# Feed-forward of a diffusion-transformer layer on one core: the hi and lo parts of four quarters of the gated features are made in the first stage and kept in DRAM

## The chip, the core and the metric

The kernel runs on one core of a Trainium2 chip. A core has a matrix engine (PE, with its weight loads shown apart as PEld), a vector engine (DVE), an activation engine (ACT), a general engine (POOL), a queue engine that issues the transfers (SP), and 16 DMA engines that carry them. The metric is the device time of one execution in microseconds; the median over several runs counts, and lower is better.

## The reference, cut to what matters

One layer (attention, then a gated feed-forward) over 1024 tokens plus 256 context tokens, in float32, width 1024; the hidden width of the feed-forward is 2816. The attention does not change. The part at hand is

```
FFN_HIDDEN = -(-8 * D_MODEL // (3 * 256)) * 256      # 2816

def _swiglu(h, w_ffn_in, w_ffn_out):
    gate, up = jnp.split(h @ w_ffn_in, 2, axis=-1)
    return (jax.nn.silu(gate) * up) @ w_ffn_out
```

Behind it come the gated residual and a last RMS norm over the 1024 features of every token.

## The kernel before, in words

**Three products for one.** A float32 matrix product is made from three fast ones: each operand is split into a high part (rounded to the fast format, `ACT.activation(hi, src, Copy)`, L344) and a low part (`DVE.tensor_tensor(lo, src, hi, subtract)`, L347), and hi·hi, hi·lo and lo·hi are summed in PSUM. So each block of 128x512 that becomes an operand costs one ACT and one DVE instruction; this is `split`.

**Seven products for eight.** Both feed-forward matrices are worked in quarters with a seven-product scheme (`p1` to `p7`). Some products take a quarter as it is, others take sums or differences of quarters, which POOL and DVE make first.

**First stage (class `Hidden`).** The hidden width is cut into 22 chunks `j` of 128. Each j has seven products of 12 matmuls (`product`, L1427). Two weight tiles `wf` of 512 KB are loaded ahead and split. At `p7` DVE (L1528, L1532, L1533) and POOL (L1532, L1533) make two gated halves `hd` [128 x 512], one for each half of the tokens; for j below 11 POOL subtracts the first from the second (L1537). Each half is stored in DRAM (`hidD`, L1538). j = 0 and 1 are written out by hand in program order (`manual_schedule`); from j = 2 on only PE's order is that of the program, and a scheduler places the instructions of DVE, ACT, POOL and SP.

**Output stage.** The products come in the order p1, p5, p2, p6, p3, p7, p4. Each runs over 11 chunks of the hidden width, and over 4 blocks of output features (`chunk_product`, L1713): 132 matmuls, 12 for a chunk. The chunks are prepared in pairs (6 pairs, the last has one chunk), three pairs ahead of their use. `prepare(name, s)` takes the left side (`left`: weights of `w_ffn_out`, loaded raw by L1635 into a ring of 512 KB tiles named wf, wh and wl) and the right side (`right`: a raw pair of `hidD` halves), and splits every chunk of either side into blocks `wh, wl, xh, xl` from a ring of 32, which is eight chunks' worth. For p5 POOL sums two raw weights into `Y` (L1662) and the right side goes into a tile `X` that is kept (L1678). For p6 POOL takes a raw weight from `Y` (L1666) and DVE makes `X` the difference of a raw half and `X` (L1682). For p3 and p7 POOL subtracts `Y` from a raw weight (L1669); for p7 and p4 DVE subtracts the raw half from `X` (L1685). p4 keeps its left parts in the `Y` tiles and a ring tile.

**What follows a product.** `take` reads the four PSUM banks: residual sums on DVE (L1728 `res`), copies on ACT, sums `y` on POOL (L1750), squares on ACT (L1298) that POOL adds up (`acc`, L1300) for the norm. After p2 POOL also scales 256-column pieces of `res` ahead of the norm (`prescale`, L1760). `stat` (L1310) sums the squares on PE in the midst of p4, after the eighth chunk of its first two feature blocks; `spread_stat` (L1321) spreads the result.

**What sets the order.** Each engine works off its instructions in order, so one that waits holds up all behind it. SP issues all transfers that matter here, also in order: a store that waits for its data holds up the loads behind it. A transfer also waits for the one issued eight places before it on SP, as they share eight semaphores.

Of the kernel before, what the change touches and what calls it, by code (L numbers as in the profile page):

```python
# [305 lines left out]
def tile_hybrid_diffattn_mla_dit_layer(  # L306
# [78 lines left out]
    VB = dram.tile([10, P, HB * 128], F32, name="VB")  # L385
    nlD = dram.tile([D, NL], F32, name="nlD")
    hidD = dram.tile([NJ, P, NL], F32, name="hidD")

    def fetch_w(src, width, kk=8):

# [1031 lines left out]
    def product(ps, w, name):  # L1422

        for k in range(4):
            xh, xl = parts[(*name, k)]
            for i, (a, b) in enumerate(((w[0], xh), (w[0], xl), (w[1], xh))):
                PE.matmul(ps, a[:, k, :], b, start=k == 0 and i == 0, stop=k == 3 and i == 2)  # L1427

    class Hidden:


# [93 lines left out]
        def p7(self):  # L1525
            d = mm_tile()
            product(d, self.s3, ("T3",))
            DVE.tensor_tensor(self.v, self.v, d, ALU.add)  # L1528
            both = []
            for i, (eng, other, op, gate) in enumerate(((DVE, self.e, ALU.subtract, self.sg0), (POOL, self.v5, ALU.add, self.sg1))):  # L1530
                hd = self.tile("hd", 3)
                eng.tensor_tensor(hd, self.v, other, op)  # L1532
                eng.tensor_tensor(hd, hd, gate, ALU.mult)  # L1533
                both.append(hd)
                if i and self.j < NJ // 2:
                    hd = self.tile("hd", 3)
                    POOL.tensor_tensor(hd, both[1], both[0], ALU.subtract)  # L1537
                dma(hidD[self.j, :, i * 512:i * 512 + 512], hd)  # L1538

    p4, pk = ExitStack(), ExitStack()  # L1540
    with tc.manual_schedule(engines=ENGINES):
# [68 lines left out]
            h.p4()  # L1610
        for h in first:
            h.p7()
    for j in range(2, NJ - 1):
        h, ahead = ahead, Hidden(j + 1)
        for step in ("p1", "p5", "p2", "p6", "p3", "p4", "p7"):
            getattr(h, step)()

# [26 lines left out]
    def hidden(a, b, s, tag=None):  # L1646
        return raw(hidden_src(a, b, s), pairs[s][1], tag)
# [24 lines left out]
    def right(name, s):  # L1672

        n = pairs[s][1]
        last = name == "p4" and ("wf", "raw")[s % 2]
        if name == "p5":
            X[s] = sum_tile("X", n)
            dma(X[s], hidden_src(0, 1, s))  # L1678
            return X[s]
        r = hidden(*{"p1": (0, 0), "p2": (1, 0), "p6": (1, 1), "p3": (1, 1), "p7": (0, 0), "p4": (1, 0)}[name], s, last)  # L1680
        if name == "p6":
            DVE.tensor_tensor(X[s], r, X[s], ALU.subtract)  # L1682
            return X[s]
        if name in ("p7", "p4"):
            DVE.tensor_tensor(r, X[s], r, ALU.subtract)  # L1685
        return r

    ready = {}

    def prepare(name, s):  # L1690

        c, n = pairs[s]
        a, b = left(name, s), right(name, s)
        if name == "p4":
            hi = sum_tile("Y", n, F32R)
            tag = RAW[2 + s % 2]
            lo = ring.tile([P, 8, P], F32R, tag=tag, name=tag, bufs=3).rearrange("p a b -> p (a b)")
            lo = lo.rearrange("p (c t) -> p c t", c=2)
        for i in range(n):
            wh, wl = (hi[:, i], lo[:, i]) if name == "p4" else (block(), block())  # L1700
            split(wh, wl, a[:, i])
            xh, xl = block(), block()
            split(xh, xl, b[:, i])
            ready[name, c + i] = wh, wl, xh, xl

    def chunk_product(name, c, ps, ds, t0=0):
# [72 lines left out]
    AHEAD = 3  # L1779
    for step in ("p1", "p2", "p5", "p6", "p3", "p4", "p7"):  # L1780
        getattr(ahead, step)()
        if step in ("p2", "p5"):
            prepare(*todo.pop(0))
        if step == "p3":
            pk.close()
            fo2 = pool(ctx, "fo2", side="right")
    p4.close()
    fo = pool(ctx, "fo")
    while len(todo) > len(order) * len(pairs) - AHEAD:
# [110 lines left out]
```

## Time and the profile before

| | |
|---|---|
| median of 3 runs | 1641.59 us (1640.61 to 1644.83) |
| the profiled execution | 1640.7 us, its span 1638.9 us, mean granted clock 0.978 |
| PE busy | 1519.1 us, 93% of the span |
| DVE, ACT, POOL busy | 1193.3, 759.6, 798.5 us |
| first stage | until 1391.95 us |
| output stage | from 1391.95 us to the end |

The span runs from the first instruction to the last of one execution; the profiled time is 1.8 us longer. A granted clock of 1.00 is 2.4 GHz on PE, 0.5 would be 1.2 GHz.

### The profile page before, as it was taken

To read this page: it belongs to the slowest core of one execution; us is meant where nothing else is said; L and a number is where in the kernel's file an instruction comes from. 1 tells how busy PE (TensorE), PEld (TensorE's weight loads), DVE (VectorE), ACT (ScalarE), POOL (GpSimd) and SP (SyncE) were. 2 spreads that over 40 slices of the span, in tenths; PEclk is the share of its full clock that TensorE was granted. 3 is DMA by queue.
4 is the path that set the end of the run, shared out by engine and by line. 5 is a ranking of instruction groups with operands and counts; after the bars stand their busy time and mean duration, and the time that the engine had idled before them with its cause. 6 is when DMAs were issued, how large, how long until landed. Compare 5 with 4: busy or idle time off the path is not lost.

```text
span 1638.9 us, 20678 instructions
## 1 busy us (share of the span) xinstructions
PE 1519.1 (93%) x7323; PEld 1214.8 (74%) x7323; DVE 1193.3 (73%) x1642; ACT 759.6 (46%) x1192; POOL 798.5 (49%) x551
## 2 busy tenths in 40 slices
PE   4899999987778899999999989999999999999887
PEld 2577888765566678788877857888888888888766
DVE  5757565579999988999975588655555556869893
ACT  5443421265556557677764444333333333444251
POOL 2435335435656656755622275755544441437531
PEclk8999999999999999999999989999999999999997
DMA  8436987592332345453217412322222225963432
GB/s 252 138 96 223 319 280 226 186 265 87 84 90 72 71 97 142 110 157 82 65 52 212 154 45 71 110 90 84 77 84 78 77 78 185 369 235 136 159 116 103
DMA packets 153923, 227.70 MB, mean 139 GB/s; under 512 B 11215, under 2 KB 80859, under 8 KB 153819
## 3 DMA queue, kind: packets, MB, share of 16 engines
q1 hardware_dynamic: 153547, 226.11, 44.7%
q8 instruction: 58, 0.95, 0.2%
q14 instruction: 46, 0.38, 0.1%
q10 hardware_dynamic: 272, 0.26, 0.0%
HBM read 172.53 MB, written 53.81 MB: 138 GB/s over the span
## 4 chain that ended last, share of the span: by engine, by line
PE 58%; DVE 23%; DMA 6%; issue 4%; POOL 4%; ACT 3%; SPq 1%; DVEq 0%; ACTq 0%; POOLq 0%
PE mm L1427 24%; PE mm L1713 8%; PE S L1056 7%; DVE nm L1076 4%; PE T L1118 4%; DVE nm L1072 4%; PE mm L1355 3%; DVE pl L1126 3%; PE acc L1135 2%; DVE block L347 2%; PE acc L1140 2%; PE mm L410 2%; PE mm L600 1%; DVE nmc L1068 1%; PE ps L1355 1%
## 5 line engine op out<-in xcount | busy, mean ns | idle before, releaser
L1090 ACT ACTIVATE e<-S,nm 128x1280 f32<-128x1280 f32 x128 | 170.1, 1329 | 104.3 <-DVE nm L1076 79.9
L1056 PE MATMUL S<-kt,qt 128*128 128x512 f32 (+1 forms) x768 | 200.9, 370 | 13.6 <-ACT e L1090 11.4
L1713 PE MATMUL mm<-block 128*128 128x512 f32 x792 | 182.0, 392 | 6.8 <-DVE block L347 6.8
L1118 PE MATMUL T<-ident,e 128*128 128x128 f32 x960 | 147.8, 277 | 36.1 <-DVE pl L1126 32.1
L1713 PEld LDWEIGHTS mm<-block 128*128 128x128 f32 x792 | 149.5, 189 | 39.1 <-DVE block L347 8.1
L1122 ACT ACTIVATE ph<-T 128x512 fp32r<-128x512 f32 x240 | 142.1, 597 | 75.8 <-PE T L1118 71.7
L1118 PEld LDWEIGHTS T<-ident,e 128*128 128x128 f32 x960 | 115.1, 142 | 77.6 <-issue 29.9
L1126 DVE TENSOR_TENSOR pl<-T,ph 128x512 fp32r<-128x512 f32 x240 | 161.3, 682 | 15.0 <-ACT ph L1122 12.5
L1056 PEld LDWEIGHTS S<-kt,qt 128*128 128x128 f32 x768 | 132.2, 192 | 49.6 <-ACT e L1090 26.3
L1072 DVE TENSOR_REDUCE nm<-S 128x1 f32<-128x1024 f32 x128 | 155.8, 1217 | 15.6 <-PE S L1056 14.3
L1110 POOL TENSOR_SCALAR e<-e,ls 128x1280 f32<-128x1280 f32 x64 | 85.9, 1342 | 116.5 <-DVE ls L1107 101.0
L1135 PE MATMUL acc<-ph,vt 128*128 128x512 f32 x320 | 131.1, 450 | 2.0 <-ACT ph L1122 1.1
L1427 PE MATMUL mm<-fresh,wh 128*128 128x512 f32 x352 | 113.8, 402 | 3.3 <-DVE fresh L1580 2.9
L1427 PE MATMUL mm<-block,wh 128*128 128x512 f32 x352 | 112.3, 400 | 0.0
L1532 POOL TENSOR_TENSOR hd<-acc,v 128x512 f32<-128x512 f32 x22 | 29.6, 1344 | 147.3 <-DVE acc L1528 135.7
L344 ACT ACTIVATE wh<-wf 128x1024 fp32r<-128x1024 f32 (+1 forms) x51 | 52.2, 1026 | 103.6 <-issue 64.1
L1140 PE MATMUL acc<-pl,vt 128*128 128x512 f32 x240 | 99.3, 414 | 0.0
L1300 POOL TENSOR_TENSOR acc<-acc,sq 128x512 f32<-128x512 f32 x23 | 35.2, 1530 | 129.6 <-ACT sq L1298 129.0
L410 PE MATMUL mm<-hH,wh 128*128 128x512 f32 (+1 forms) x256 | 95.2, 372 | 0.0
L1104 POOL TENSOR_TENSOR e<-e,e 128x1280 f32<-128x1280 f32 x32 | 93.6, 2926 | 2.7
L410 PE MATMUL mm<-hH,wl 128*128 128x512 f32 (+1 forms) x256 | 93.9, 367 | 0.0
L410 PE MATMUL mm<-hL,wh 128*128 128x512 f32 (+1 forms) x256 | 93.8, 366 | 0.0
(367 smaller groups left out, 3705.5 us busy)
## 6 DMA issues: line engine op xcount, KB each, us to landing
wf<-in_w_ffn_in_dram SPq DMA_DIRECT2D x44, 512.0 KB, 3.8
hidD<-hd SPq DMA_DIRECT2D x44, 256.0 KB, 2.1
wh<-in_w_ffn_out_dram SPq DMA_DIRECT2D x21, 512.0 KB, 5.9
wl<-hidD SPq DMA_DIRECT2D x17, 512.0 KB, 6.5
wa<-in_w_ada_dram SPq DMA_DIRECT2D x16, 512.0 KB, 4.0
wa<-in_w_ada_dram SPq DMA_DIRECT2D x32, 256.0 KB, 3.7
qt<-QB SPq DMA_DIRECT2D x32, 256.0 KB, 4.4
qt<-QA SPq DMA_DIRECT2D x32, 256.0 KB, 4.9
```

Source lines behind the costliest of these rows:

```text
L410: PE.matmul(ps, a(k), b(k), start=start and i == 0, stop=stop and i == n - 1)
L1056: m = PE.matmul(S[:, c0:c0 + w], q, k[:, k0:k0 + w], start=s == 0, stop=s == len(job) - 1)
L1072: on_banks(DVE.tensor_reduce(self.stats(n)[0][:, i:i + 1], sl, AX.X, ALU.max, negate=True), BANKS[i], DVE)
L1090: m = ACT.activation(e, S[:, i * NT:(i + 1) * NT], AF.Exp, bias=self.s[n][0][:, i:i + 1], accum_out=total)
L1104: POOL.tensor_tensor(self.e[n, 0], self.e[n, 0], self.e[n, 1], ALU.add)
L1118: PE.transpose(self.T[c][:, b * P:(b + 1) * P], e[:, kc * P:(kc + 1) * P], ident)
L1122: ACT.activation(self.ph[c], self.T[c], AF.Copy)
L1126: DVE.tensor_tensor(self.pl[c], self.T[c], f32(self.ph[c]), ALU.subtract)
L1135: PE.matmul(self.acc[u, qh, j], vt[:, kc, v], self.ph[c], start=kc == 0 and i == 0, stop=False)
L1140: PE.matmul(self.acc[u, qh, j], self.kv[u][1][:, kc, v], self.pl[c], start=False, stop=kc == 9)
L1427: PE.matmul(ps, a[:, k, :], b, start=k == 0 and i == 0, stop=k == 3 and i == 2)
L1713: PE.matmul(ps[d], w[:, sl], x[:, t0:t0 + n], start=c == 0 and i == 0, stop=c == NH - 1 and i == 2)
```

## The change

The kept DRAM tile `hidS` gets, for each of the 44 halves `hd`, its high and low part side by side. A new function `split_late` makes them with one `split` into a tile `hs` of two blocks and stores it (512 KB). It is called after p1 and after p5 of the next j; for j = 0 and 1 it stands right behind each `p7`, within the part that is ordered by hand; for the last j it is called after p1, p5 and p7. `hd` has two buffers instead of three, as POOL now subtracts in place.

In the output stage p1, p2, p5 and p3 take quarters of the features as they are (`PLAIN`). For these `prepare` loads `xh` and `xl` straight from `hidS` into blocks (two transfers of 256 KB for a chunk) and splits nothing on that side. p6, p7 and p4 take differences and are as before; `X` is still loaded for p5.

```
+    hidS = dram.tile([NJ, P, 2, 2, 512], F32, name="hidS")
...
+    late = []
+
+    def split_late():
+
+        if late:
+            hd, dst = late.pop(0)
+            hs = ff.tile([P, 2, 512], F32R, tag="hs", name="hs", bufs=1)
+            split(hs[:, 0], hs[:, 1], hd)
+            dma(dst, f32(hs))
...
-                hd = self.tile("hd", 3)
+                hd = self.tile("hd")
                 eng.tensor_tensor(hd, self.v, other, op)
                 eng.tensor_tensor(hd, hd, gate, ALU.mult)
                 both.append(hd)
                 if i and self.j < NJ // 2:
-                    hd = self.tile("hd", 3)
-                    POOL.tensor_tensor(hd, both[1], both[0], ALU.subtract)
+                    POOL.tensor_tensor(hd, hd, both[0], ALU.subtract)
                 dma(hidD[self.j, :, i * 512:i * 512 + 512], hd)
+                late.append((hd, hidS[self.j, :, i]))
...
         for h in first:
             h.p7()
+            while late:
+                split_late()
...
             getattr(h, step)()
+            if step in ("p1", "p5"):
+                split_late()
...
-        if name == "p5":
-            X[s] = sum_tile("X", n)
-            dma(X[s], hidden_src(0, 1, s))
-            return X[s]
-        r = hidden(*{"p1": (0, 0), "p2": (1, 0), "p6": (1, 1), "p3": (1, 1), "p7": (0, 0), "p4": (1, 0)}[name], s, last)
+        r = hidden(*{"p6": (1, 1), "p7": (0, 0), "p4": (1, 0)}[name], s, last)
...
+    PLAIN = {"p1": (0, 0), "p2": (1, 0), "p5": (0, 1), "p3": (1, 1)}
...
-        a, b = left(name, s), right(name, s)
+        a = left(name, s)
+        if name == "p5":
+            X[s] = sum_tile("X", n)
+            dma(X[s], hidden_src(0, 1, s))
+        if name not in PLAIN:
+            b = right(name, s)
...
             xh, xl = block(), block()
-            split(xh, xl, b[:, i])
+            if name in PLAIN:
+                half, i2 = PLAIN[name]
+                for p, t in enumerate((xh, xl)):
+                    dma(f32(t), hidS[half * NH + c + i, :, i2, p])
+            else:
+                split(xh, xl, b[:, i])
...
         getattr(ahead, step)()
+        if step in ("p1", "p5", "p7"):
+            split_late()
...
+    while late:
+        split_late()
     p4.close()
```

In total 44 splits leave the output stage and 44 enter the first one, so the engines' instruction counts stay the same (1056 activations, 1044 two-operand DVE instructions, 7142 matmuls). SP issues 750 transfers instead of 636: 44 stores of 512 KB and 88 loads of 256 KB come in, and 18 raw loads of `hidD` (8.25 MiB) fall away.

How the change moves the rows is shown at three places. The line numbers of the changed kernel are 12 to 24 higher (L1528 became L1540, L1666 became L1682, L1760 became L1784).

First DVE, where j = 0 and 1 end and j = 2 begins. `acc` (L1528) adds p7's bank, `hd` (L1532, L1533) makes the gated half, `wl`, `sl` and `ul` are low parts of weights, `y` is the gate of j = 2. Before:

```order
L1528 TENSOR_TENSOR acc<-acc,mm 128x512
L347 TENSOR_TENSOR wl<-wf,wh 128x1024
L1532 TENSOR_TENSOR hd<-acc,mm 128x512
L1533 TENSOR_TENSOR hd<-hd,y 128x512
L1528 TENSOR_TENSOR acc<-acc,mm 128x512
L1532 TENSOR_TENSOR hd<-acc,mm 128x512
L347 TENSOR_TENSOR ul<-wf,uh 128x512
L1533 TENSOR_TENSOR hd<-hd,y 128x512
```

And in the changed kernel:

```order
L1540 TENSOR_TENSOR acc<-acc,mm 128x512
L347 TENSOR_TENSOR wl<-wf,wh 128x1024
L1544 TENSOR_TENSOR hd<-acc,mm 128x512
L1545 TENSOR_TENSOR hd<-hd,y 128x512
L347 TENSOR_TENSOR hs<-hd,hs 128x512
L347 TENSOR_TENSOR ul<-wf,uh 128x512
L347 TENSOR_TENSOR sl<-s_9274,sh 128x1024
L1511 TENSOR_TENSOR y<-acc,mm 128x512
L347 TENSOR_TENSOR wl<-s_9275,wh 128x1024
L347 TENSOR_TENSOR hs<-hd,hs 128x512
L1540 TENSOR_TENSOR acc<-acc,mm 128x512
```

The second `acc`, that of j = 1, which frees its PSUM bank, now stands behind both `hs` of j = 0 and behind four instructions that belong to j = 2.

Next SP at the passage from the first stage to the output stage, in the changed kernel: `hidS<-hs` are the stores of the last parts, `block<-hidS` the loads of p1's and then p5's right side, `X`, `wf`, `wh`, `wl` raw loads of p5.

```order
L1651 DMA wl<-in_w_ffn_out_dram 128x2x512
L1549 DMA hidD<-hd 128x512 x2
L1439 DMA hidS<-hs 128x1024
L1725 DMA block<-hidS 128x512 x4
L1439 DMA hidS<-hs 128x1024
L1725 DMA block<-hidS 128x512 x3
L1744 DMA res<-nlD 128x2x512 x2
L1725 DMA block<-hidS 128x512
L1710 DMA X_12363<-hidD 128x2x512
L1725 DMA block<-hidS 128x512 x4
L1651 DMA wf<-in_w_ffn_out_dram 128x2x512 x2
```

Before, two stores of `hidD` stood here among raw loads; now two stores of `hidS` do as well, and the last of them stands ahead of p1's last blocks and of all of p5's.

Last POOL from p6's differences to p3's. Before:

```order
L1666 TENSOR_TENSOR Y_12445<-Y_12445,wh 128x512
L1669 TENSOR_TENSOR wf<-wf,Y_12203 128x1024
L1669 TENSOR_TENSOR wh<-wh,Y_12251 128x1024
L1669 TENSOR_TENSOR wh<-wh,Y_12299 128x1024
L1669 TENSOR_TENSOR wh<-wh,Y_12349 128x1024
L1760 TENSOR_SCALAR res<-res,fnorm 128x256 x2
L1300 TENSOR_TENSOR acc<-acc,sq 128x512
L1760 TENSOR_SCALAR res<-res,fnorm 128x256 x2
```

And in the changed kernel:

```order
L1682 TENSOR_TENSOR Y_12453<-Y_12453,wh 128x1024
L1784 TENSOR_SCALAR res<-res,fnorm 128x256 x2
L1302 TENSOR_TENSOR acc<-acc,sq 128x512
L1784 TENSOR_SCALAR res<-res,fnorm 128x256 x2
L1302 TENSOR_TENSOR acc<-acc,sq 128x512
L1784 TENSOR_SCALAR res<-res,fnorm 128x256
L1302 TENSOR_TENSOR acc<-acc,sq 128x512
L1784 TENSOR_SCALAR res<-res,fnorm 128x256
L1682 TENSOR_TENSOR Y_12503<-Y_12503,wh 128x1024
L1682 TENSOR_TENSOR Y_12551<-Y_12551,wf 128x1024
L1682 TENSOR_TENSOR Y_12599<-Y_12599,wh 128x512
```

Before, all six differences of p6 and four of p3 were made ahead of the scaling and the sums of squares that belong to p2's results; now the differences of p6's pairs 3 to 5 stand behind them.

## Rows read from the trace of the kernel before

**Rows 1.** The page, part 1: busy time, share, instructions of each engine.

```profile
PE 1519.1 (93%) x7323; PEld 1214.8 (74%) x7323; DVE 1193.3 (73%) x1642; ACT 759.6 (46%) x1192; POOL 798.5 (49%) x551
```

**Rows 2.** Windows: stretch, length, busy time by engine, PE clock, DMA share, GB/s.

```profile
1160.00:1200.00 40.00, 40.00 (x175) 32.64 (x174) 22.30 (x25) 13.01 (x17) 21.23 (x15) 1.00 0.26 88
...
1392.00:1422.00 30.00, 30.00 (x134) 24.86 (x133) 25.36 (x26) 13.70 (x25) 17.26 (x8) 1.00 1.00 363
1422.00:1453.00 31.00, 31.00 (x139) 25.67 (x138) 18.57 (x28) 15.79 (x29) 2.09 (x2) 1.00 0.81 291
1453.00:1483.00 30.00, 30.00 (x134) 24.86 (x133) 27.21 (x22) 11.88 (x21) 16.70 (x7) 1.00 0.61 204
1483.00:1514.00 31.00, 31.00 (x139) 25.67 (x138) 31.00 (x33) 15.74 (x28) 27.37 (x14) 1.00 0.39 142
1514.00:1545.00 31.00, 25.51 (x107) 20.66 (x106) 25.73 (x31) 7.65 (x14) 13.70 (x7) 0.94 0.46 160
...
1599.00:1639.00 40.00, 31.81 (x167) 27.45 (x167) 15.24 (x34) 5.59 (x12) 6.92 (x9) 0.80 0.30 105
```

**Rows 3.** Timeline of PE, output stage: start, length, line, count, idle before and releaser.

```profile
1391.95 136.39 PE L1713 MATMUL mm<-block 128*128 128x512 f32 x601
1533.83 31.66 PE L1713 MATMUL mm<-block 128*128 128x512 f32 x132 [5.49 <-DVE block L347]
1566.79 13.97 PE L1713 MATMUL mm<-block 128*128 128x512 f32 x59 [1.30 <-DVE block L347]
```

**Rows 4.** Timeline of PE around the sums of squares in p4.

```profile
1599.23 1.87 PE L1310 MATMUL mm<-ones,acc 128*128 128x2 f32 x8 [7.37 <-POOL acc L1300]
...
1602.66 1.20 PE L1713 MATMUL mm<-block,Y 128*128 128x512 f32 x2
```

**Rows 5.** The chain that ended last, in order of time: start, length, what.

```profile
999.05 393.06 PE mm L1427 x1703
...
1536.14 4.54 DMA wl<-hidD
...
1624.05 1.23 PE mm L1310 x12
```

**Rows 6.** Groups by line and shape, 1060 to 1392 us: busy, mean ns, idle before.

```profile
L1533 DVE TENSOR_TENSOR hd<-hd,y 128x512 f32<-128x512 f32 x17 | 30.2, 1778 | 0.0
...
L347 DVE TENSOR_TENSOR ul<-wf,uh 128x512 fp32r<-128x512 f32 x16 | 12.2, 760 | 9.2 <-ACT uh L344 9.2
...
L344 ACT ACTIVATE uh<-wf 128x512 fp32r<-128x512 f32 x16 | 10.2, 635 | 6.4 <-PE mm L1427 6.4
```

**Rows 7.** DMA from 1390 to 1430 us: GB/s by slice of 1 us; one group of issues.

```profile
GB/s 201 301 385 406 406 363 166 287 125 254 348 375 381 406 369 410 401 381 379 391 391 385 389 389 379 391 387 389 383 385 389 389 387 387 381 389 387 389 391 383
...
wl<-hidD SPq DMA_DIRECT2D x3, 512.0 KB, 8.8
```

**Rows 8.** The page, part 6: transfers, count, KB each, median us to landing.

```profile
wf<-in_w_ffn_in_dram SPq DMA_DIRECT2D x44, 512.0 KB, 3.8
hidD<-hd SPq DMA_DIRECT2D x44, 256.0 KB, 2.1
```

**Rows 9.** Timeline of DVE where j = 1 ends and j = 2 begins.

```profile
1010.71 0.68 DVE L1528 TENSOR_TENSOR acc<-acc,mm 128x512 f32<-128x512 f32 x1
1012.25 0.69 DVE L1532 TENSOR_TENSOR hd<-acc,mm 128x512 f32<-128x512 f32 x1 [0.86 <-POOL hd L1537]
```

**Rows 10.** Timeline of POOL in the output stage.

```profile
1394.67 1.64 POOL L1533 TENSOR_TENSOR hd<-hd,sq 128x512 f32<-128x512 f32 x1
...
1451.77 2.42 POOL L1666 TENSOR_TENSOR Y<-Y,wh 128x1024 f32<-128x1024 f32 x1 [28.91 <-DMA wh<-in_w_ffn_out_dram]
...
1494.23 2.85 POOL L1760 TENSOR_SCALAR res<-res,fnorm 128x256 f32<-128x256 f32 x2
1497.04 1.72 POOL L1300 TENSOR_TENSOR acc<-acc,sq 128x512 f32<-128x512 f32 x1
```

**Rows 11.** Instructions of L1713 by operation: duration ns min/median/max.

```profile
L1713 PEldq EVENT_SEMAPHORE  x1: 51/51/51, 1387.9 to 1387.9; - x1
```

## The prediction

> **What bounds the kernel now.** I read the page's totals first: PE is busy for 93% of the span [rows 1], so what can be won is the rest, where PE waits or runs slowly. Next the chain that ended last. From 999.05 us it stays on PE for 393 us without a break [rows 5]: the first stage is bound by matmuls alone, and the DVE, ACT and DMA work beside them costs nothing. The windows say how much room lies beside them: in 40 us of the first stage DVE is busy for 22.3 us, ACT for 13.0, POOL for 21.2, the DMA engines for 26% at 88 GB/s [rows 2].
>
> In the output stage the timeline of PE shows where it stands still [rows 3, 4]. It runs 601 matmuls without a gap (136.39/601 = 0.2269 us each), waits 5.49 us for a DVE split in p3 (the 601 matmuls are four products of 132 and 73 of the next), waits 1.30 us for another in p7, and waits 7.37 us in p4 for POOL's sums of squares. Up to that point DVE is the engine without a pause: 27.2 us of 30 in p2, 31.0 of 31 in p6 [rows 2]. So p3's wait is the end of a backlog on DVE that builds from p2 on. The clock falls with the waits: 0.94 in the window of the 5.49 us and 0.80 at the end [rows 2].
>
> **How much could go at most.** The waits up to p7: 5.49 + 1.30. The matmuls after them are slower than 0.2269 us: 31.66 − 132 × 0.2269 = 1.71 and 13.97 − 59 × 0.2269 = 0.58. Together 9.1. In p4: the 7.37 us; then sixteen small matmuls from 1599.23 to 1602.66, 3.43 us, where the same kind later takes 1.23/12 = 0.10 each [rows 4, 5], so 1.8 too many; and the matmuls right behind run at half the clock (1.20 us for a pair that is 0.62 elsewhere), about 2.5 us more for the dozen up to the norm's spread. Together 11.7. All of it is 20.8 us.
>
> **The change, term by term.**
>
> *Removed from the output stage.* 44 splits, one ACT and one DVE instruction each. In the first stage's rows a DVE low part of this shape takes 0.76 us, an ACT high part 0.635 [rows 6]. So DVE gets back 44 × 0.7 = 31 us in p1, p5, p2 and p3, 7.7 in each. p2 then needs 19.5 us of 30 on DVE and no backlog reaches p6 and p3. The 5.49 and 1.30 us with their slow matmuls go: **−9.1**. For p3 one more link counts: before, its late chunk also stood behind a load of 4.54 us whose ring tile came free late [rows 5]; with a less busy DVE it comes free sooner. The sums of squares in p4 were late because p7's results stood on DVE behind p4's preparation. With p7 on time they are taken about 8 us after p7's end (eight residual instructions and some four splits or differences between them, at the 0.69 us of such a row [rows 9]), and PE asks for them after 8 × 6 matmuls = 10.9 us. A margin of near 3 us: the wait goes, **−11.7**.
>
> *Added to the first stage.* For each j two splits: 1.3 us of ACT, 1.5 of DVE (up to 3.6 when each runs as slowly as the `hd` row, 1.78 us, beside a POOL instruction [rows 6]). A j is 84 matmuls; 393.06/1703 × 84 = 19.4 us. DVE goes from 10.8 to between 12.3 and 14.4 us of it, ACT from 6.3 to 7.6: covered by PE. Without that cover it would be 22 × 1.5 = 33 us. The 1 MiB that is stored for each j adds 54 GB/s to 88. Zero, up to a slip of a few us where j = 1 ends: there DVE now frees j = 1's bank behind both splits of j = 0 and parts of j = 2. Before, `acc` ran at 1010.71 us [rows 9]. The second split waits for the first store; a store of 256 KB takes 2.1 us and a load of 512 KB 3.8 [rows 8], and four instructions of j = 2 stand between, so I put the bank's release at about 1024. The eight banks are used in turn, so PE comes back to it after seven products of 2.77 us, near 1029. Zero is what I take; the bound is 6 us.
>
> *The passage to the output stage.* Here the DMA engines are already full: 363 GB/s on average, 389 in the steady part [rows 2, 7], and the 512 KB loads take 8.8 us. The change replaces 0.5 MiB of raw loads for a pair by 1 MiB of blocks in p1 and p2, adds 1 MiB per pair in p5, and puts the last store of `hidS` ahead of p1's last blocks and all of p5. `hd` of the last j is ready at 1394.67 + 1.64 = 1396.3 [rows 10]; the store before it, of 512 KB, takes up to 8 us in this traffic, and `hs` has one buffer: I put the last store at 1404.5. From it on, in the order of SP, 12 MiB must land until p5's seventh chunk (needed at 1392 + 30 + 6 × 2.72 = 1438.3) and 16.25 MiB until its eleventh (1449.2). At 389 GB/s they land at 1436.8 and 1448.3, a margin of 1.5 and 0.9; at 363 at 1439.2 and 1451.4, late by 0.9 and 2.2. Between the two ends I take **+1.5**. In p2 the need falls to 8.25 MiB in 30 us (288 GB/s) and the lead comes back.
>
> The Trainium skill (DMA: Bandwidth & Descriptors, section "Bandwidth") says that for transfers between HBM and SBUF it is the HBM side that binds, at about 358 GB/s for a core. The trace disagrees, as one core alone held 389 for over 15 us [rows 7], and the trace decides. By the skill's figure 16.25 MiB would land at 1452.1, and this term would be 2.9 instead of 1.5.
>
> *p6.* Its left side is `Y` less a raw weight, on POOL. For pairs 3 to 5 these differences now stand behind the scaling and the sums of p2's results: six pieces of 2.85/2 = 1.43 and three sums of 1.72 make 13.7 us [rows 10], starting some 1.5 us after p2's end E, when p2's results are first taken. Then the difference (2.42, [rows 10]) and a split by ACT and DVE (1.4): ready at E + 19.0. PE needs it after six chunks, E + 16.3. So a wait of 2.7 us that was not there; from 0, where POOL runs faster beside a less busy DVE, to 4.5. I take **+2.7** with 0.3 for the clock: +3.
>
> *Waits in PE's queue.* PE must now wait for DMA semaphores of the blocks: 41 more semaphore instructions. The one such instruction that the rows show took 0.051 us [rows 11]: from 0, where the queue of matmuls hides them all, to 2.1 us. I take the middle, **+1**.
>
> **Sum.** −9.1 − 11.7 + 1.5 + 3 + 1 = −15.3. Against the profiled 1640.7 us that gives 1625.4; the median of the runs lies 0.9 above the profiled one, so I predict **1626 us**.
>
> **Rivals.**
>
> 1. *The waits come back elsewhere.* p4's margin of 3 us is a chain on DVE, ACT and POOL in order; p6 and p7 still make differences on DVE, which worked 31 of 31 us in p6 [rows 2]. If p4's wait stays (−9.1 + 5.5 instead of the whole −15.3), the time is 1637 to 1642. For it: p7 and p4 keep all of their splits, and POOL's delay in p6 pushes every later `Y` difference back. Against it: the 31 us that DVE gets back lie ahead of p6.
>
> 2. *DMA-bound p5.* If loads of 256 KB among stores bring less than the row's rate, each chunk of p5 waits. At 330 GB/s the 16.25 MiB land at 1456.1: 7 us instead of 1.5, 1632 us. At 291 GB/s, which is what the stretch of p5 moved before (it was not asked for more) [rows 2], at 1463, 14 us: 1639. It ends on the slow side only under some 260 GB/s. Against it: the 389 of the steady part.
>
> 3. *Slower: the first stage no longer hides its work.* The two splits of each j stand on DVE and ACT in order, ahead of instructions that free PE's banks, and each waits for `hs` until the store before it has landed. If that makes PE wait by x in each of 20 j, the loss is 20x; from x = 0.8 us on nothing is left of the gain, from 1.05 us on it is slower than 1646.5. At 1.3 us, one DVE split not hidden and half of a second: 1652. For it: POOL and DVE slow each other (the 1.78 and 0.76 us of the same shape [rows 6]), and the store must go into a queue that SP works off in order. Against it: 8 us of each 19.4 in which DVE is idle [rows 2], and a chain that never leaves PE there [rows 5].
>
> 4. *All waits gone.* POOL is quicker in p6 and the DMA keeps 389 GB/s: −20.8 + 1, 1621.
>
> **How the numbers follow.** The forecast (with its own range of 1620 to 1634) 0.52; rival 4, 0.12; rival 2, 0.11, of which 0.09 still under 1636.7; rival 1, 0.14, one third of it still under 1636.7; rival 3, 0.11, of which 0.03 within 0.3%. A time within 0.3% of 1641.6 (1636.7 to 1646.5) is what a measurement of this kernel can hardly tell from no change. Faster: 0.52 + 0.12 + 0.09 + 0.04 = 0.77, which I cut to 0.74, since three of the terms rest on an order that I read without times. Same 0.15, slower 0.11. For the range I leave out rival 3 and the worst of rival 1, and what lies beyond rival 4: **1618 to 1640**.
>
> **What would show it in the profile after.** First stage: the chain stays on PE until about 1392, DVE at 25 to 27 us of 40. If its end moves by more than 3 us, rival 3 is at work. Passage: DMA full until about 1450 with the traffic above 380 GB/s, and in PE's timeline at most 3 us of waits for a DMA in p5. p6: one wait near its seventh chunk with a releaser on the way POOL `Y`, DVE block. p3, p7: no wait above 1 us. p4: no wait ahead of L1310, and sixteen small matmuls in 1.7 us. The prediction is wrong if p4's wait stays, if p6's wait is above 5 us, or if the first stage gets longer.

## The result, and the profile after

The changed kernel takes 1657.16 us (median of 6 runs, 1649.96 to 1661.56), the kernel before 1639.61 us (median of 6 runs). The ratio is 1.0101, 95% interval 1.0071 to 1.0131: slower by about 1%, outside the range of the prediction and on the other side. The profiled execution of the changed kernel took 1653.1 us (span 1651.3), at the low end of its runs, against 1640.7 (span 1638.9) before. What follows accounts for these 12.4 us; the further 4 us between this execution and the median lie in executions that were not profiled.

The windows of the changed kernel (length, then busy time of PE, PEld, DVE, ACT and POOL, PE clock, DMA share, GB/s):

```profile
1160.00:1200.00 40.00, 40.00 (x175) 32.67 (x174) 27.59 (x30) 15.73 (x23) 23.39 (x15) 1.00 0.38 137
...
1392.00:1422.00 30.00, 30.00 (x134) 24.86 (x133) 9.67 (x13) 5.18 (x9) 6.36 (x4) 1.00 0.98 354
1422.00:1453.00 31.00, 28.99 (x120) 23.12 (x119) 10.54 (x13) 7.37 (x13) 10.45 (x5) 0.94 1.05 387
1453.00:1483.00 30.00, 30.00 (x134) 24.86 (x133) 12.31 (x13) 8.96 (x17) 7.30 (x3) 1.00 1.05 387
1483.00:1514.00 31.00, 23.77 (x95) 18.53 (x93) 25.58 (x23) 10.00 (x18) 26.57 (x16) 0.89 0.62 218
1514.00:1545.00 31.00, 28.17 (x114) 23.13 (x115) 27.68 (x30) 9.86 (x17) 16.00 (x9) 0.89 0.50 164
```

Beside [rows 2] the reader sees that DVE did lose the work: 9.7, 10.5 and 12.3 us in the three stretches of p1, p5 and p2, instead of 25.4, 18.6 and 27.2. But the DMA engines are now full for three stretches instead of one, and in the fourth, where PE was solid before, it is busy for only 23.8 of 31 us. DVE's freed time lies where nothing waits for DVE, and ahead of p6 it is idle for want of data.

The timeline of PE, from the first matmul of the output stage to the sums of squares (start, length, count, idle before and releaser):

```profile
1390.97 46.49 PE L1737 MATMUL mm<-block 128*128 128x512 f32 x204
1439.45 61.94 PE L1737 MATMUL mm<-block 128*128 128x512 f32 x264 [1.99 <-DMA block<-hidS]
1505.92 0.80 PE L1737 MATMUL mm<-block 128*128 128x512 f32 x1 [4.54 <-ACT block L344]
1507.96 4.59 PE L1737 MATMUL mm<-block 128*128 128x512 f32 x12 [1.25 <-DVE block L347]
1516.83 32.82 PE L1737 MATMUL mm<-block 128*128 128x512 f32 x133 [4.28 <-DVE block L347]
1550.52 27.27 PE L1737 MATMUL mm<-block 128*128 128x512 f32 x119 [0.86 <-DVE block L347]
1578.68 13.88 PE L1737 MATMUL mm<-block 128*128 128x512 f32 x59 [0.90 <-DVE block L347]
1592.41 0.62 PE L1737 MATMUL mm<-block,Y 128*128 128x512 f32 x2
...
1611.53 1.86 PE L1312 MATMUL mm<-ones,acc 128*128 128x2 f32 x8 [4.07 <-POOL acc L1302]
```

204 matmuls are p1 and six chunks of p5: there stands a wait of 1.99 us for a load, and the 264 behind it take 61.94 − 264 × 0.2269 = 2.0 us too long. 468 are p1, p5, p2 and six chunks of p6. At 1439.45 + 61.94 = 1501.39 p6 asks for its seventh chunk, and the next 13 matmuls (2.95 us of work) last until 1516.83: 12.5 us lost at one place. Behind it 5.2 us more are lost up to the end of p7 (waits of 0.86 and 0.90, and 73.97 us for 311 matmuls that should take 70.57). But 2.6 of them (32.82 − 133 × 0.2269) belong to p6's wait as well, as PE came out of it at half its clock (windows; the clock is the number after ACT's and POOL's busy times):

```profile
1515.00:1520.00 5.00, 3.17 (x8) 2.49 (x9) 5.00 (x3) 1.64 (x4) 4.01 (x2) 0.50 0.16 61
1520.00:1525.00 5.00, 5.00 (x20) 4.08 (x19) 5.00 (x10) 3.54 (x7) 0.00 (x0) 0.84 0.37 100
```

So p6 costs 15.1 us, and p3 and p7 lose 2.5 where 9.1 were lost before. From the first matmul of p4 to the sums of squares it is 19.1 us; before it was 18.6. The balance: +4.0 in p5, +15.1 in p6, −6.6 in p3 and p7, +0.5 in p4, together +13.1 without rounding; the output stage as a whole grew from 247.0 to 260.3 us, and the first stage happened to end 1.0 us sooner in this execution.

Why p6's chunk was late shows on POOL (timeline, `Y` is p6's left side, `res` the scaling, `acc` the sums of squares):

```profile
1472.63 2.40 POOL L1682 TENSOR_TENSOR Y<-Y,wf 128x1024 f32<-128x1024 f32 x1 [24.46 <-DMA wf<-in_w_ffn_out_dram]
...
1478.03 2.50 POOL L1682 TENSOR_TENSOR Y<-Y,wh 128x1024 f32<-128x1024 f32 x1 [0.31 <-DMA wh<-in_w_ffn_out_dram]
...
1486.82 2.37 POOL L1784 TENSOR_SCALAR res<-res,fnorm 128x256 f32<-128x256 f32 x2 [6.29 <-ACT acc L1297]
...
1497.66 2.40 POOL L1682 TENSOR_TENSOR Y<-Y,wh 128x1024 f32<-128x1024 f32 x1
```

and on DVE right behind that (timeline):

```profile
1500.75 2.19 DVE L347 TENSOR_TENSOR block<-Y,block 128x512 fp32r<-128x512 f32 x1 [4.67 <-ACT block L344]
1502.87 2.28 DVE L1694 TENSOR_TENSOR X<-wl,X 128x1024 f32<-128x1024 f32 x1
...
1507.83 2.86 DVE L347 TENSOR_TENSOR block<-Y,block 128x512 fp32r<-128x512 f32 x1
1510.61 3.40 DVE L1694 TENSOR_TENSOR X<-wf,X 128x1024 f32<-128x1024 f32 x1
1513.93 2.84 DVE L347 TENSOR_TENSOR block<-X,block 128x512 fp32r<-128x512 f32 x1
```

POOL waits 24.46 us for the first raw weight of p6 and starts at 1472.63; before it started at 1451.77 [rows 10]. So only three pairs are done when p2 ends. The fourth raw weight landed at 1486.0 (issued at 1475.23, 10.8 us to landing, from the timeline of SP and the DMA view of that stretch), but its difference, at 1497.66, stood behind the scaling and the sums of squares on POOL:

```profile
1475.23 0.37 SPq L1651 DMA_DIRECT2D wh<-in_w_ffn_out_dram  x1
```

```profile
wh<-in_w_ffn_out_dram SPq DMA_DIRECT2D x1, 512.0 KB, 10.8
```

The rest of p6 is then made in one burst by POOL and DVE side by side, where DVE's splits take 2.0 to 2.9 us each instead of the 0.76 of [rows 6].

### The profile page after: what moved, and what is told of

Read it like the earlier page. It is cut to its first block, busy times and chain, and to the rows that moved or that the text cites. A ratio compares the mean times of both kernels' runs of the same rounds, so it can differ in the third digit from the quotient of the medians.

```text
span 1651.3 us, 20896 instructions
## 1 busy us (share of the span) xinstructions
PE 1529.2 (93%) x7323; PEld 1223.1 (74%) x7323; DVE 1191.7 (72%) x1642; ACT 755.4 (46%) x1192; POOL 803.1 (49%) x551
## 4 chain that ended last, share of the span: by engine, by line
PE 54%; DVE 21%; DMA 10%; issue 4%; ACT 4%; POOL 4%; SPq 1%; POOLq 0%; ACTq 0%; DVEq 0%
PE mm L1429 24%; PE S L1058 7%; DVE nm L1078 4%; PE T L1120 4%; DVE nm L1074 4%; PE mm L1737 3%; PE mm L1357 3%; DVE pl L1128 3%; DMA block<-hidS 2%; PE acc L1137 2%; PE acc L1142 2%; PE mm L412 2%; PE mm L602 2%; DVE nmc L1070 1%; PE ps L1357 1%
## 5 line engine op out<-in xcount | busy, mean ns | idle before, releaser
L1737 PE MATMUL mm<-block 128*128 128x512 f32 x792 | 187.8, 399 | 13.8 <-DVE block L347 7.3
L1128 DVE TENSOR_TENSOR pl<-T,ph 128x512 fp32r<-128x512 f32 x240 | 161.4, 682 | 13.4 <-ACT ph L1124 11.2
L344 ACT ACTIVATE hs<-hd 128x512 fp32r<-128x512 f32 x44 | 27.8, 632 | 151.1 <-DMA hidS<-hs 95.0
L347 DVE TENSOR_TENSOR hs<-hd,hs 128x512 fp32r<-128x512 f32 x44 | 38.6, 876 | 79.1 <-ACT hs L344 79.1
```

The lines of the kernel that those rows point to most:

```text
L1128: DVE.tensor_tensor(self.pl[c], self.T[c], f32(self.ph[c]), ALU.subtract)
L1737: PE.matmul(ps[d], w[:, sl], x[:, t0:t0 + n], start=c == 0 and i == 0, stop=c == NH - 1 and i == 2)
```

## The experiments

All times are medians; the kernel before ran beside each group, with medians of 1641.4 (e1 to e4), 1642.0 (e5 to e8), 1641.2 (e9 to e12), 1642.7 (e13 to e16) and 1640.3 us (e17, e18). Two theories were set against each other at the outset: A, the order that the scheduler chose for POOL and DVE costs the time; B, the traffic of the block loads does. C puts it on the first stage. From e5 on, "the program's own order" means one added line ahead of the output stage's loop:

```
+    ctx.enter_context(tc.manual_schedule(engines=ENGINES))
     for name in order[:-1]:
```

**e1: the first stage's part alone.** `PLAIN = {}`; all parts are written, none is loaded.

> All 44 splits and stores of hidS are made in the first stage, but the output stage loads and splits raw halves as before the change. Theory A (POOL's order in p6 costs the time) and theory B (the traffic of the block loads costs it) both expect no change against the kernel before, 1638 to 1643 us, with the first stage's chain of matmuls at 393 us. Theory C (the first stage no longer hides its added work) expects 1645 us or more and a first stage that ends later.

1640.38 us, ratio 0.9997 (0.9978 to 1.0015). C falls. Groups of the first stage by shape (e1, 1060 to 1392 us; busy, mean ns, idle before), and its chain:

```profile
L347 DVE TENSOR_TENSOR hs<-hd,hs 128x512 fp32r<-128x512 f32 x35 | 29.4, 839 | 66.3 <-ACT hs L344 66.3
...
L344 ACT ACTIVATE hs<-hd 128x512 fp32r<-128x512 f32 x35 | 22.1, 632 | 127.8 <-DMA hidS<-hs 79.5 <-DVE hd L1545 24.4 <-issue 20.9
```

```profile
1000.31 393.08 PE mm L1429 x1703
```

The added splits cost 0.84 and 0.63 us each and wait for their own store, and the 1703 matmuls take 393.08 us as before [rows 5].

**e2: half of the bytes.** Only the high parts are loaded.

```
-            xh, xl = block(), block()
+            xh = block()
+            xl = xh if name in PLAIN else block()
...
-                for p, t in enumerate((xh, xl)):
-                    dma(f32(t), hidS[half * NH + c + i, :, i2, p])
+                dma(f32(xh), hidS[half * NH + c + i, :, i2, 0])
```

> For p1, p2, p5 and p3 only the high part is loaded from hidS, and the same block stands in for the low part (so the result lacks the low parts of these features): 11 MiB less is loaded in the output stage, and no split comes back. POOL's order, which the scheduler chooses anew, has all six of p6's differences ahead of the scaling again. A and B: no wait for a DMA in p5, p6's wait at its seventh chunk below 2 us, p4's wait near 7 us as it stands, 1629 to 1634 us. If it stays above 1640 us, neither the order nor the traffic is the cause.

1637.77 us, ratio 0.9981 (0.9964 to 0.9998). No wait in p5 and p6, as expected; but the gain is 3.6 us and not 8 to 12. POOL's order differs here too (all six differences of p6 stand ahead of the scaling), so e2 does not tell traffic from order. p3 waits again, 2.38, 0.69 and 0.81 us, and p4's sums still wait 7.49 us. So with half of the bytes gone, 44 splits less are worth a few us and not the 20.8 of the prediction's ceiling.

**e3: the scaling moved out of p6.**

```
+    f2 = tmp.tile([P, 4], F32, name="f2")
+    DVE.scalar_tensor_tensor(f2, V[3][:, 0:4], 0.0, fnorm[:, 0:4], ALU.mult, ALU.add)
...
-        POOL.tensor_scalar(y, y, fnorm[:, d:d + 1], 1.0, ALU.mult, ALU.mult)
+        POOL.tensor_scalar(y, y, f2[:, d:d + 1], 1.0, ALU.mult, ALU.mult)
```

> The changed kernel, but the six scalings on POOL read a copy of the gains that is made (exactly) behind p6's results, so that they cannot stand in p6. Traffic as in the changed kernel. A: p6's wait falls from 12.5 us in all to 3 to 5 us (three sums of squares still stand ahead of the last differences), the time falls by 6 to 10 us to 1644 to 1650. B: p6's raw loads come as late as before, its wait stays at 10 us or more, the time stays within 3 us of the changed kernel's 1657.

1659.13 us, ratio 1.0109 (1.0083 to 1.0135). A's number is missed by 9 us or more: p6 still waits 2.46, 1.36, 1.54 and 4.48 us although no scaling stands in front. The three sums of squares still do, and they wait for their own data (timeline of POOL):

```profile
1489.86 3.00 POOL L1302 TENSOR_TENSOR acc<-acc,sq 128x512 f32<-128x512 f32 x2 [9.26 <-ACT sq L1300]
...
1494.52 2.85 POOL L1682 TENSOR_TENSOR Y<-Y,wh 128x1024 f32<-128x1024 f32 x1
```

The fourth difference starts 3.1 us sooner than in the changed kernel, and PE's waits in p6 are 9.8 us in all against 10.1. So the scaling by itself is not what p6's wait comes from. What part the sums in front have, e3 does not say.

**e4: p2 and p3 alone.** `PLAIN = {"p2": (1, 0), "p3": (1, 1)}`, and only these quarters are split early.

> Only p2 and p3 load their parts from hidS (22 splits moved instead of 44, only j from 11 on); p1 and p5 load raw halves and split them as before the change. The DMA engines are not full in p2 and p3. A and B: p5 without a DMA wait, p6's wait below 2 us, p3's 5.49 us gone, p4's wait stays: 1630 to 1636 us, faster than the kernel before. If DVE was not what held p3 up: 1639 or more.

1645.77 us, ratio 1.0010 (0.9989 to 1.0032): a miss for both theories. No wait in p5 and p6, but p3 waits 7.33 us for a block's load where it waited 5.49 us for a split before. The wait has changed its name and not gone.

**e5 to e8: the program's own order.** e5 is the kernel before, e6 the changed kernel, e7 has p2 and p3 alone; e8 is the changed kernel with this order only from the start of p7 on, which takes in p4's preparation.

> The kernel before the change, but DVE, ACT and POOL work in the program's own order through the whole output stage, not in the scheduler's; work and traffic are the same. Theory A (orders cost the time): p7's results are taken on DVE as soon as PE has them, p4's wait of 7.37 us and its clock go, 1628 to 1634 us. Theory B (traffic, and loads that come late): the order is not what p4 waits for, 1638 to 1645 us.

> The changed kernel with the program's own order in the output stage. Traffic as in the changed kernel. A: p6's 12.5 us fall below 3 us as well as p4's wait; what stays is p5's 4 us of DMA wait and clock: 1626 to 1632 us, not slower than the kernel before in the same order. B: p6's raw loads still land some 20 us later than before the change; p6 waits 8 us or more, and it is slower than the kernel before in the same order by 8 us or more.

> Only p2 and p3 load their parts (22 splits moved), with the program's own order in the output stage. A: no wait in p5 and p6, p3's and p4's gone: 1623 to 1629 us, the fastest of these. B: p3's wait for a DMA (7.3 us with the scheduler's order) stays at 4 us or more, 1634 us or more.

> The changed kernel with the program's own order from p7's results on, and the scheduler's order ahead of it (which has the six scalings at the end now, but still the three sums ahead of p6's last differences). A: only p4's wait goes, 11 us off the changed kernel: 1644 to 1649 us. B: p4's wait is for its own late loads: 1654 us or more.

e5: 1646.48 us, ratio 1.0028 (1.0015 to 1.0042). e6: 1650.21, 1.0056 (1.0039 to 1.0074). e7: 1642.25, 0.9994 (0.9977 to 1.0012). e8: 1652.60, 1.0057 (1.0044 to 1.0071). A is wrong for e5, and B's upper end is passed by 1.5 us: taking the results first does away with the wait for the sums of squares, but p3 then waits 8.52 us, and p4's own splits are late. e6 lies between the theories; its p6 still waits 2.46 and 2.53 us. e7 misses A's number by 13 us; p3 waits 8.85 us in it, for a split and not for a load as B had it. e8 gains 4.6 us on the changed kernel and not 8 or more, as 4.71 us of wait for a split of p4 take the place of the sums'. In one order, moving 22 splits (e7) gains 4.2 us on moving none (e5), and moving 44 (e6) loses 3.7.

**e9 to e12: the sums that stand between p6 and p3.** The two residual loads and the four sums on DVE were moved in the program:

```
-        if name == "p6":
+        if name == "p3":
             for i in (2, 3):
                 load_res(i, 0, "p5")
             for d in range(4):
                 add_to(d + 4, 0, V[d])
```

e9 is the kernel before with this, e10 the changed one, e11 has p2 and p3 alone, e12 is e11 with the program's own order from the start of p7 on.

> The kernel before the change, with one edit: the two residual loads into tiles that p5's results leave, and the four sums on DVE that use them, stand behind p3's results in the program, not behind p6's. Theory D (p3's wait is not a backlog of splits but a chain behind p6: POOL's y frees the tile, then a load of 3.6 us, then the four sums on DVE, and p3's splits only then): the 5.49 us and the slow matmuls behind go, 1632 to 1637 us. The reading of the prediction (a backlog of splits on DVE since p2): no change, 1639 to 1644 us.

> The changed kernel with the same edit. D: nothing changes in p5 and p6 (12.5 us), as p6's wait lies ahead of it; p3's remaining waits are small in the changed kernel already: 1650 to 1657 us.

> Only p2 and p3 load their parts, with the same edit. D: the load for p3 that stood on SP behind the residual loads (7.33 us of wait) is free, no wait above 1.5 us up to the end of p7; p4's wait stays: 1633 to 1638 us, about as e9. If the 22 splits that left p2 and p3 are worth anything by themselves, it is faster than e9 by 2 us or more.

> As e11, with the program's own order of DVE, ACT and POOL from p7's results on. If the sums of squares in p4 wait only because DVE takes p7's results behind p4's preparation, their wait goes here, 6 to 10 us less than e11: 1625 to 1631 us. If p4's own loads are too late (its ring tiles come free one pair at a time), the wait goes over to p4's matmuls, and it is within 3 us of e11.

e9: 1642.30 us, ratio 0.9999 (0.9984 to 1.0014). e10: 1658.17, 1.0090 (1.0068 to 1.0112). e11: 1641.79, 0.9991 (0.9975 to 1.0007). e12: 1640.34, 0.9984 (0.9970 to 0.9997). e9 and e11 do not decide on theory D, as the scheduler set the two loads on SP where they had stood. In e9 p3's wait falls to 0.98 and 1.98 us, and p7's rises from 1.30 to 4.27. e10 lies 1 us above its range. e11 misses D's number by 4 us, and the 22 splits gain nothing clear in it (0.9991 against e9's 0.9999). It does show what p3 waits for there. SP's own waits in e11 from 1490 to 1540 us (waited for, us in total, times, longest), then PE:

```profile
SPq L1745 <- POOL y L1775: 9.7, 2, 7.5
```

```profile
1536.18 43.17 PE L1738 MATMUL mm<-block 128*128 128x512 f32 x180 [7.59 <-DMA block<-hidS]
```

SP stands for 9.7 us at the residual loads, which wait for POOL's `y`, and the load of a block of p3 that PE waits for stands behind them. e12 is within 3 us of e11: PE no longer waits for the sums, but 4.26 us for p4's own split. So p4 is held up by its own preparation as much as by the order of p7's results. Of the kernels that leave nothing out, e12 alone has an interval that lies below 1, by 0.5 to 5 us; among this many runs that can be chance.

**e13: the residual loads off SP.** In the kernel of e4 POOL issues them itself.

```
+        (POOL.dma_start if tag == "p5" else dma)(r, nlD.rearrange(...))
-        dma(r, nlD.rearrange(...))
```

> Only p2 and p3 load their parts, in the scheduler's order; the two residual loads into the tiles that POOL's y frees are issued by POOL itself, so that SP no longer stands at them for 9.5 us with p3's blocks behind. Theory E (p3's wait is a load that stands behind a waiting load on SP): the 7.33 us go, 1635 to 1639 us. If p3 is held by DVE all the same, a wait of 4 us or more for a DVE split takes its place: 1641 us or more.

1645.88 us, ratio 1.0023 (1.0008 to 1.0039). Theory E falls: the load's wait goes to below 1.2 us, but PE waits for a split at the same place.

```profile
1536.14 4.39 PE L1738 MATMUL mm<-block 128*128 128x512 f32 x10 [5.36 <-DVE block L347]
```

**e14: the traffic by itself.** e6 with e2's edit. In the two traces the matmuls stand in the same order, and so do the rows of DVE, ACT and POOL but for a handful ahead of the output stage's loop.

> The changed kernel in the program's own order as in e6, with only the high parts loaded (the same block stands in for the low part, so the result lacks the low parts of these features). POOL, DVE and ACT do the same work in the same order as in e6, and 11 MiB less is loaded. Theory B (traffic): p5's 3.44 us and p6's 5 us of waits go with the clock lost there, 8 to 12 us less than e6: 1638 to 1642 us. Theory A: within 3 us of e6, 1647 to 1653 us.

1637.53 us, ratio 0.9979 (0.9965 to 0.9993): 12.7 us less than e6, a little more than B's 8 to 12. The timelines of PE and POOL in e6:

```profile
1440.01 63.39 PE L1737 MATMUL mm<-block 128*128 128x512 f32 x265 [3.44 <-DMA block<-hidS]
1505.85 3.02 PE L1737 MATMUL mm<-block 128*128 128x512 f32 x12 [2.46 <-DVE block L347]
1511.40 4.54 PE L1737 MATMUL mm<-block 128*128 128x512 f32 x12 [2.53 <-DVE block L347]
```

```profile
1474.01 2.40 POOL L1682 TENSOR_TENSOR Y<-Y,wf 128x1024 f32<-128x1024 f32 x1 [25.38 <-DMA wf<-in_w_ffn_out_dram]
```

and in e14:

```profile
1390.25 111.68 PE L1737 MATMUL mm<-block 128*128 128x512 f32 x492
```

```profile
1449.92 2.41 POOL L1682 TENSOR_TENSOR Y<-Y,wf 128x1024 f32<-128x1024 f32 x1 [14.79 <-DMA wf<-in_w_ffn_out_dram]
```

With the bytes gone p6's first raw weight is there 24 us sooner, and PE runs 492 matmuls (p1, p5, p2 and eight chunks of p6) without a stop. The edit also takes away 44 transfers and a fourth of the blocks of p1, p5, p2 and p3. That these and not the bytes free p6 is unlikely, as the DMA share is 1.03 from 1422 to 1483 us in e6, that is, the engines are full; but no run parts the two.

**e15 and e16: all three edits** (the program's own order, the sums moved, the residual loads on POOL) with p2 and p3's parts loaded, and without any part of the change.

> Only p2 and p3 load their parts; the program's own order in the output stage; the residual loads are issued by POOL and the four sums on DVE that need them stand behind p3's results. E: p3's waits (1.18 and 8.85 us in e7) fall below 2 us, p4's stay as in e7: 1632 to 1637 us. If the waits only move on, 1640 us or more.

> The kernel before with the same three edits as e15 but without any part of the change: raw halves are loaded and split. If the 22 splits off DVE are worth something once p3's chain is gone, e15 is 2 us or more faster than this; if the chain was all, the two are equal within 2 us. 1634 to 1642 us.

e15: 1644.79 us, 1.0010 (0.9993 to 1.0028). e16: 1649.52, 1.0049 (1.0032 to 1.0067). They lie 7.8 and 7.5 us above their ranges. p3's wait is down to 1.70 us in e15, but p7's seventh chunk is late instead, as the sums now stand in front of its preparation:

```profile
1570.33 16.70 PE L1738 MATMUL mm<-block 128*128 128x512 f32 x60 [8.17 <-ACT block L344]
```

The 22 splits are again worth 4.7 us between two kernels of one order.

**e17 and e18: without p5's part.** `PLAIN` without p5, whose 11 chunks are split from the kept `X` as before; e17 in the scheduler's order, e18 in the program's own.

> The changed kernel without p5's part: p5 splits its kept X as before (11 splits come back to the output stage, 5.5 MiB less is loaded where the DMA engines are full), the scheduler's order. B: p5's wait for a DMA goes, p6's raw loads land some 14 us sooner and its 12.5 us fall below 3: 1639 to 1645 us. If it stays above 1652 us, the bytes in p5 are not what holds p6 up.

> As e17 with the program's own order in the output stage, beside e6 (all four loaded) and e14 (half of the bytes). B: between the two, nearer to e14: 1638 to 1643 us, no wait in p5 and less than 2 us in p6. If the order was what counted: as e6, 1648 to 1653 us.

e17: 1647.91 us, 1.0041 (1.0029 to 1.0054). e18: 1638.74, 0.9990 (0.9975 to 1.0005). In both p6's wait is gone: 408 matmuls (p6 included) run on in e17, and in e18 the two waits in p6 are below 0.3 us. Its PE, up to p6's eighth chunk:

```profile
1437.38 65.36 PE L1738 MATMUL mm<-block 128*128 128x512 f32 x287 [0.53 <-DVE block L347]
```

e18 is 11.5 us faster than e6 by this one edit. In e17 the order has changed as well, the fourth difference standing ahead of the scaling there, so that the comparison of e18 with e6 is the clean one. e17 misses its number by 3 us, as p5 waits 3.43 us for a split and p3 6.86 us for a block's load. p6's first difference, in e17 and in e18:

```profile
1467.57 2.55 POOL L1683 TENSOR_TENSOR Y<-Y,wf 128x1024 f32<-128x1024 f32 x1 [30.34 <-DMA wf<-in_w_ffn_out_dram]
```

```profile
1454.78 2.44 POOL L1683 TENSOR_TENSOR Y<-Y,wf 128x1024 f32<-128x1024 f32 x1 [20.53 <-DMA wf<-in_w_ffn_out_dram]
```

The program's own order, side by side (medians; the profile's p1 to p7, from the first matmul of the output stage to the first of p4, where 792 × 0.2269 = 179.7 us would be no wait at all; p6's waits from its seventh chunk on):

| splits moved | loads added | run | us | p1 to p7 | p6's waits |
|---|---|---|---|---|---|
| 0 | none | e5 | 1646.5 | 197.5 | 0.2 |
| 22 (p2, p3) | 5.5 MiB | e7 | 1642.3 | 192.8 | 0.2 |
| 33 (p1, p2, p3) | 8.25 MiB | e18 | 1638.7 | 194.3 | 0.5 |
| 44 (all) | 13.75 MiB | e6 | 1650.2 | 206.8 | 5.2 |
| 44, half of the bytes | 2.75 MiB | e14 | 1637.5 | 193.2 | 0.6 |

The loads added are the blocks' bytes less the raw loads that fall away. By the ratios to the kernel before, p2's and p3's parts gain in this order (0.9994 against 1.0028), p1's gains nothing that the runs can tell (0.9990), and p5's, which has no raw load to save since `X` is loaded all the same, costs 11 us (1.0056 against 0.9990). In the scheduler's order no part gains: e4 lies at 1.0010, e17 at 1.0041.

## Why the prediction was wrong

In short, −15.3 us were predicted and +12.4 came. The largest error is p4 (−11.7 against +0.5), next p6 (+3 against +15.1). Two of the signs that the prediction named for being wrong came: p4's wait stayed, and p6's was above 5 us.

**The first stage: right.** Zero was predicted; e1 measures 0.9997. DVE was put at 12.3 to 14.4 us of a j; 27.59/40 × 19.4 is 13.4. No stall showed where j = 2 begins; the chain of the changed kernel stays on PE as before:

```profile
998.07 393.07 PE mm L1429 x1703
```

**The passage: the mechanism right, the size off, and its reach not seen.** The wait stands at p5's seventh chunk, where the margin was put at 1.5 us. It costs 4.0 us with its slow matmuls, against 1.5. The traffic held its rate over some 60 us, which the DMA view of the changed kernel from 1390 to 1470 us shows (GB/s by slice of 2 us):

```profile
GB/s 348 366 404 397 416 361 209 283 322 249 360 390 385 391 387 391 384 389 384 389 388 383 390 384 388 385 390 388 383 387 385 390 386 386 388 386 387 389 377 386
```

The Trainium skill's 358 GB/s (DMA: Bandwidth & Descriptors, section "Bandwidth") is exceeded again: from 1412 us on every slice but one lies at 383 to 391. The same section gives the 358 as the share of a core when both cores of an HBM domain stream, and up to 425 for one alone; the trace of this one core agrees with that. What failed is the sentence "In p2 the need falls to 8.25 MiB in 30 us (288 GB/s) and the lead comes back." The arithmetic counted p2's own loads only. Behind them, on the same queue, stand p6's raw loads, which work on two more engines must follow; these came 20.9 us later (1472.63 against 1451.77).

**p6: the term of +3 was 15.1, mis-sized behind a mechanism that was there.** The fourth difference did stand behind the scaling and the sums of p2's results, and was even done sooner than put (1500.06 = E + 15.0, E being 1501.39 − 72 × 0.2269 = 1485.05, against E + 17.6). But behind it came 16.8 us of preparation up to the second of the two late chunks, not 1.4: two differences of `X` on DVE as well, and each DVE instruction two to four times as long beside POOL's burst. The clock took 2.6 us more, where 0.3 was put. That so much was left to do after p2 comes from the late raw loads: e14 and e18 stay in the program's own order, as e6, with the sums ahead of the fourth difference; they take bytes away, and the wait goes. So in that order p6's wait is shown to need the traffic. The scaling alone is shown not to make it (e3). But the order has a part: with the first raw weight as late (1474.01 against 1472.63) p6 waits 5.2 us in e6 and 10.1 in the changed kernel. Which link of the order that is stays open, as no run with all the bytes has the late differences ahead of the sums.

**p3 and p7: −9.1 was −6.6, in part by luck, and the reading behind it was wrong.** PE came to p3 19 us later for its own losses in p5 and p6, which gave p3's preparation that time. "So p3's wait is the end of a backlog on DVE that builds from p2 on" does not hold: with 44 splits and half of the bytes gone p3 still waits 10.26 us in e14 and 3.9 in e2.

```profile
1538.59 45.00 PE L1737 MATMUL mm<-block 128*128 128x512 f32 x190 [10.26 <-DVE block L347]
```

Between p6 and p3 stands a round trip, DVE to POOL's `y` to DVE four times, a load into a tile that `y` frees, and four more sums. Moving single links of it (e9, e11, e13, e15) moved the wait to another name or to p7. Which link is the least that has to go was not found.

**p4: −11.7 was +0.5.** This is the largest single error. "A margin of near 3 us" assumed that DVE takes p7's results 8 us after p7's end. DVE in the changed kernel (timeline, `res` the first of p7's results):

```profile
1604.16 1.22 DVE L1697 TENSOR_TENSOR wf<-X,wf 128x1024 f32<-128x1024 f32 x1
1605.29 0.69 DVE L347 TENSOR_TENSOR wl<-raw,Y 128x512 fp32r<-128x512 f32 x1
1605.89 0.75 DVE L1752 SCALAR_TENSOR_TENSOR res<-mm,modF,res 128x512 f32<-128x512 f32 x1
```

And in the kernel before:

```profile
1593.59 0.74 DVE L1728 SCALAR_TENSOR_TENSOR res<-mm,modF,res 128x512 f32<-128x512 f32 x1
```

It takes them at 1605.89, 13.5 us after p4 began at 1592.41; before, it was 13.0 (1593.59 after 1580.60). In front stands p4's preparation, and that waits for a load, which the chain of the changed kernel names:

```profile
1593.84 7.21 DMA wf<-in_w_ffn_out_dram
```

This load can only be issued when a pair before it has left one of two `wf` tiles. So p4 is a string of load, split and load, tied to its few raw tiles, and the change does not touch them. The prediction counted the DVE instructions in front and not the loads that they wait for. e12 shows that putting the results in front gains little, as p4's splits are then late by themselves.

**PE's semaphores: +1 was near 0.** The first 204 matmuls take 46.49 us, 0.2 more than at 0.2269 each.

**The rivals.** Rival 3 (the first stage) fell with e1. Rival 2 had the right resource and the wrong place: full DMA engines cost p5 4 us, and they led to p6's 15.1. Rival 1, that p4's wait stays, came true besides.

## What to carry to other kernels

Taking work from a busy engine pays only where its next result is what the bound engine waits for; "released by DVE" names the last link, and the reader has to ask what DVE itself waited for (a load, another engine's sum, a tile that comes free late) before the freed time is counted as gain. When a queue of transfers is driven to its limit, work out the landing time not only of the next product's loads but of the first load behind them whose data must still pass through other engines: here the lag was paid there, after the traffic had ended. Where a quarter of a change has no saving of its own on the limited resource (p5's part, whose `X` is loaded anyway), try the change without it.

## What the runs showed of the hardware

A DVE split of 128x512 took 0.69 us where POOL was idle and 2.0 to 2.9 us while POOL worked through its differences without a pause; a DVE difference of 128x1024 1.2 and 2.3 to 3.4 us. The Trainium skill (GPSIMD Engine Reference, section "Key points") says that GpSimd shares its SBUF interfaces with VectorE and contends with DVE instructions that have two SBUF inputs; the trace agrees, with a factor of up to four that I had not put into the sum. Which of the two pays differs: at 1554.64 in the changed kernel POOL's difference took 5.84 us, not 2.4, while DVE's splits beside it ran at 0.68 each. Over the whole span the change did not make this dearer: DVE was busy for 1191.7 us, against 1193.3 [rows 1], with the same instructions. What changed is where the long ones fall.
